# Output weights' operands made in two large tiles of their own, spread over more products, and more gate buffers in the merging

## The chip, the cores and the metric

The kernel runs on one core of a Trainium2 chip. The metric is the device time of one execution in microseconds (us). The time of before is the median of three runs; its profile is one further execution, taken by the hardware profiler.

## The reference

One mixer layer over two sequences (1024 and 256 tokens, width 1024, all float32): a normed and modulated input `h` goes through one wide projection, whose slices feed two branches; the branches are merged by gates and projected once more.

```
p = h @ w_in                         # 1024 -> 11280 columns
y_conv = cb * dwconv3(cc * cx) * silu(cz)
h_fwd, h_bwd = mlstm(q, k, v, gates), the same on the flipped sequence
y_m = sigmoid(o) * headnorm(h_fwd + h_bwd) * silu(mz)
g_conv, g_mlstm = split(sigmoid(gmerge))
merged = g_conv * (y_conv @ w_proj_conv) + g_mlstm * (y_m @ w_proj_mlstm)
y = rms_norm(x + gate * (merged @ w_out))
```

## The kernel before, in words

**Numbers.** The matmuls take float32r operands. To keep float32's accuracy each operand is split into a high part (rounded by a cast) and a low part (what is left), and a product is hi·hi + hi·lo + lo·hi. A split of weights is `split_op`: ACT casts the raw values into `wh` (L319), POOL subtracts to make `wl` (L320). `wh` and `wl` have four buffers each in the pool `wp`, taken in turn: the fifth split gets the first buffer, when what used it is done.

**The order.** The kernel doesn't issue instructions directly. Each piece of work is recorded with `op` (engine, an assumed duration, what it reads and writes, a step, and `low` for work without hurry) on a `Board`. When a stage is written, the board plays all its pieces through a simple model of the engines and issues them in the order of the modelled starts. On the chip each engine (and SP, which issues the DMAs) then works off its own list strictly in order; a piece that is late holds all that stands behind it on that engine. `board.step` says at which product a piece is due.

**The in-projection.** The columns of `w_in` go in pairs of 128-column blocks. A pair is a one-level Strassen product of seven half-size products (moving operands `b11`, `b21`, `t2`, `t3`, `t1`, `t4`, `b22`; the hi and lo parts of these lie in tiles named `b00H`, `b00L`, `b10H`, `t2H`, `xt` and so on); some gate pairs have five after their corners were done first. All stand in the list `todo`: 308 products. `go(k)` issues product k: 24 matmuls of 128x128 by 128x320 into one `acc` (L809; three `acc` buffers in PSUM). `prep(k)` makes its weights some products ahead: raw loads, combinations on DVE (L674), the split. The result is read out of `acc` by DVE (L718) or ACT (L732). `advance(n)` runs `go` for the products from `at[0]` to n and sets `at[0]` to n. `ends[0]` is 77 (the gate pairs and the first head's K, V and Q are done), `ends[1]` 84 (behind the first of eight output-gate pairs, `og`), `ends[2]` 91, `ends[8]` 133; the pairs of the convolution branch follow.

**Beside the products.** Several jobs are put between them, all in this one stage:
- `out_weights` makes the operands for the last projection: it loads `w_out`, forms the seven Strassen combinations, splits them, and stores them in DRAM (`op_dr`, seen in the trace as `b_dr` and `t_dr`) until the end. In before it does so in four steps. Each loads 4 × 256 KB into two tiles of the pool `big` (two buffers), and has eight parts: an ACT cast (L1293, 128x512) into a `wh`, a POOL subtraction (L1294) into a `wl`, and two stores of 256 KB (L1297). DVE makes the combinations in place (L1300). One part is put at each product, from 36 on.
- `gate_inputs` makes the 16 gate columns by a small product of its own (L988, 64 matmuls of 128x32 by 128x320), with both `big` and one `wh`.
- `recurrences` computes the chunk recurrences of the gates, and `weights(i)`, twenty times, loads a row from DRAM (`a_dr`) into a `big`, works on it on POOL and ACT, and stores it (`ex_dr`). The combinations of the convolution pairs use `big` too.

**Merging.** `merge(i, y)` is run for 16 blocks near the end: it loads a gate tile `th` and a tile `zc` of 128x640 (320 KB each), multiplies 24 matmuls per half into a PSUM bank (L1869 to L1871), then DVE multiplies (L619) and adds `zc` (L1877). `th` has three buffers, `zc` two. The raw weights of the blocks come in pairs of loads (`raw`, three buffers), and `b`, `t` tiles of the last projection's operands come back from DRAM in the same queue. `th` tiles are also the landing places in the mLSTM stage before it (L1682) and in `first_ym` and `second_ym`.

The driving loop of the in-projection in before:

```
    beginning()
    advance(31)
    for _ in out_weights():
        advance(at[0] + 1)
    advance(ends[0] - 7)
    board.step = at[0]
    gate_inputs()
```

`out_weights` yields 40 times, so the loop ends with `at[0]` at 71; `advance(70)` then runs nothing and sets it to 70.

Of the kernel before, what the change touches and what calls it, by code (L numbers as in the profile page):

```python
# [9 lines left out]
F32 = mybir.dt.float32  # L10
# [6 lines left out]
P = 128  # L17
# [12 lines left out]
TH2 = T // 2  # L30
TQ = T // 4
SEQS = [(0, 8), (8, 2)]
CB, CC, CX, CZ, CQ, CK, CV, CO, CMZ, CGP, CGM = (
# [7 lines left out]
class Board:  # L41
# [140 lines left out]
def encoder_kernel(  # L182
# [124 lines left out]
    def load(kb, dst, src, r, w, low=False):  # L307
        op("SP", kb, lambda: dma(dst(), src), r=r, w=w, low=low)
# [296 lines left out]
    def big():  # L605

        return buf(rp, [P, T], F32, "big", 2)
# [667 lines left out]
    def out_weights():  # L1275

        for k in range(4):
            places = [big() for _ in range(2)]
            r11, r12, r21, r22 = raws = [((lambda b=places[i % 2], c=i // 2: b[:, c * 512:(c + 1) * 512]), (places[i % 2], i // 2))
                                         for i in (0, 1, 2, 3)]  # L1280
            for i, (ap, tok) in enumerate(raws):
                kt, n0 = k + 4 * (i // 2), 512 * (i % 2)
                load(256, ap, w_out[0, kt * P:(kt + 1) * P, n0:n0 + 512], (), [tok], True)

            for _ in range(1 + 4 * (k == 0)):
                yield

            def parts(nm, x):
                wh, wl = (buf(wp, [P, 4, P], F32R, t, 4) for t in ("wh", "wl"))
                def flat(t):  # L1290
                    return t[:].rearrange("p a b -> p (a b)")

                op("ACT", .63, lambda: A.copy(flat(wh), x[0]()), r=[x[1]], w=[wh])  # L1293
                op("POOL", 1.4, lambda: G.tensor_tensor(out=flat(wl), in0=x[0](), in1=fp(flat(wh)), op=ALU.subtract),  # L1294
                   r=[x[1], wh], w=[wl])
                for i, t in enumerate((wh, wl)):
                    op("SP", 256, lambda i=i, t=t, k=k: dma(op_dr[nm][i, :, k], fp(flat(t))), r=[t], low=True)  # L1297

            def comb(out, x, y, o=ALU.subtract):
                op("DVE", .69, lambda: V.tensor_tensor(out=out[0](), in0=x[0](), in1=y[0](), op=o), r=[x[1], y[1]], w=[out[1]])  # L1300

            yield parts("b22", r22)
            yield parts("b12", r12)
            comb(r22, r22, r12)
            yield parts("t3", r22)
            yield parts("b11", r11)
            comb(r12, r12, r11)
            yield parts("t1", r12)
            yield parts("b21", r21)
            comb(r11, r22, r11, ALU.add)  # L1310
            yield parts("t2", r11)
            comb(r21, r21, r11)
            yield parts("t4", r21)
# [68 lines left out]
    psB = bstack.enter_context(tc.tile_pool(name="psB", bufs=3, space=PSUM))  # L1382
    thp = hpstack.enter_context(tc.tile_pool(name="thp", bufs=3, side="right"))

# [244 lines left out]
    class Filler:  # L1629
# [36 lines left out]
        def unit(self, after):  # L1666
# [6 lines left out]
            if q == 0:  # L1673
                if 0 < i < 2 * KT - 1:
                    self.split(i + 1)
                if i % 2 == 0 and i < 2 * KT - 2:
                    self.load_w(i // 2 + 1)
                if i == KT:
                    self.load_y(1)
                t0 = HBS[b][0]  # L1680
                if i:
                    self.th[i] = buf(thp, [P, TH2], F32, "th", 3)  # L1682
                    load(320, lambda i=i: self.th[i][:], th_dr[n * P:(n + 1) * P, t0:t0 + TH2], (),
                         [(self.th[i], 0), (self.th[i], 1)])
# [21 lines left out]
    def first_ym(n):  # L1706
# [3 lines left out]
        for k in range(4):  # L1710
            raw = buf(thp, [P, TH2], F32, "th", 3)
            kt = 4 * n + k
# [81 lines left out]
    mgp = ctx.enter_context(tc.tile_pool(name="mgp", bufs=1))  # L1794
    zcp = hpstack.enter_context(tc.tile_pool(name="zcp", bufs=2, side="right"))
    banks = []
# [31 lines left out]
    def second_ym(n):  # L1828
        y = [buf(hp, [P, 4, TH2], F32R, ("b00", "b10")[n] + part, 1) for part in "HL"]
        v = ym_dr[:].rearrange("(k p) t -> p k t", p=P)  # L1830
        for k in range(4):
            raw = buf(thp, [P, TH2], F32, "th", 3)
            kt = 4 * n + k
# [464 lines left out]
```

## Time and profile before

| what | us |
|---|---|
| median of 3 runs (1697.9 to 1701.9) | 1698.43 |
| the profiled execution | 1700.25 |
| its span (first to last instruction) | 1698.5 |
| PE busy | 1640.0 |
| DVE, ACT, POOL busy | 1031.7, 584.8, 704.7 |

The stages lie so in the span: preparation to about 87 us, in-projection to about 1180, mLSTM with the convolution branch's projection to about 1460, merging to about 1590, then the last projection. The output weights are made between about 165 and 320.

The profile's page lists busy time, a picture of the span in 40 slices, the chain of work that ended last, and groups of instructions. The views of the trace that are used here: *waits* list, for each engine, what its instructions waited for (total us, times, longest us); *windows* give the busy time of each engine in a stretch, with the clock that TensorE was granted (1.00 is full), the share of time that the DMA engines were busy, and GB/s; the *timeline* gives single instructions with start, length and, in brackets, the idle time ahead of them and what ended it. PE is the matmul part of TensorE, PEld its weight loads.

### The profile page before, as it was taken

Reading aid. Unit: us, or ns where it says so; the run is one execution under the profiler, and the core shown is the slowest. Engines: PE = TensorE matmul, PEld = TensorE weight load, DVE = VectorE, ACT = ScalarE, POOL = GpSimd, SP = SyncE. Lnnn points to the kernel's source line nnn. Section 1 sums busy time; section 2 is a strip of 40 time slices with the busy share of each in tenths; the row PEclk is TensorE's granted clock in tenths of the full one; section 3 lists DMA queues with packets and bytes.
Section 4 is the critical chain, followed back from the end, with each engine's and each line's share of the span. In section 5 each row is a group of like instructions: output and inputs, shape, how many; then the busy total and the mean of one; then the engine's idle time right before and its main releaser. Section 6 shows DMA issues by size and latency. Waiting matters only on the chain.

```text
span 1698.5 us, 28022 instructions
## 1 busy us (share of the span) xinstructions
PE 1640.0 (97%) x10528; PEld 1564.9 (92%) x10528; DVE 1031.7 (61%) x1731; ACT 584.8 (34%) x1142; POOL 704.7 (41%) x514
## 2 busy tenths in 40 slices
PE   6999999899999999999999999999999999999997
PEld 3989998799999999999999999999888899999876
DVE  5785555456645656666565887752147777443587
ACT  4643443124544222222222222121256565321232
POOL 1243665434655466776666643333210002333000
PEclk8999999999999999999999999999999999999999
DMA  9434769523554122222222465557878865795654
GB/s 362 131 98 153 246 225 253 124 83 104 152 149 127 49 74 81 69 61 66 74 69 69 121 148 147 118 128 241 286 237 259 273 196 165 256 325 191 227 190 161
DMA packets 300746, 275.44 MB, mean 162 GB/s; under 512 B 98260, under 2 KB 240836, under 8 KB 300612
## 3 DMA queue, kind: packets, MB, share of 16 engines
q1 hardware_dynamic: 300308, 273.40, 52.2%
q8 instruction: 83, 1.36, 0.3%
q14 instruction: 51, 0.42, 0.1%
q10 hardware_dynamic: 304, 0.27, 0.0%
HBM read 187.94 MB, written 85.66 MB: 161 GB/s over the span
## 4 chain that ended last, share of the span: by engine, by line
PE 75%; DMA 2%; DVE 2%; ACT 1%; SPq 0%; issue 0%; POOL 0%; ACTq 0%; DVEq 0%
PE acc L809 50%; PE u L1486 3%; PE qc L1446 3%; PE acc L1961 2%; PE acc L1962 2%; PE acc L1963 2%; PE acc L1694 2%; PE acc L1693 2%; PE acc L1869 2%; PE acc L1695 2%; PE acc L1870 2%; PE acc L1871 2%; DMA th<-th_dr 1%; PE misc L1569 1%; PE misc L1529 1%; PE acc L988 1%
## 5 line engine op out<-in xcount | busy, mean ns | idle before, releaser
L320 POOL TENSOR_TENSOR wl<-comb,wh 128x512 fp32r<-128x512 f32 x176 | 251.5, 1430 | 257.7 <-ACT wh L319 236.3
L320 POOL TENSOR_TENSOR wl<-raw,wh 128x512 fp32r<-128x512 f32 x169 | 237.8, 1408 | 274.7 <-ACT wh L319 258.9
L718 DVE TENSOR_TENSOR q<-acc,q 128x640 f32<-128x640 f32 x272 | 220.5, 818 | 193.2 <-PE acc L809 185.0
L809 PE MATMUL acc<-xt,wh 128*128 128x320 f32 x1408 | 264.8, 310 | 2.0 <-ACT wh L319 2.0
L809 PEld LDWEIGHTS acc<-xt,wh 128*128 128x128 f32 x1408 | 221.7, 188 | 2.6 <-ACT wh L319 2.5
L319 ACT CAST wh<-raw 128x512 fp32r<-128x512 f32 x169 | 104.2, 619 | 310.6 <-PE acc L809 181.9
L319 ACT CAST wh<-comb 128x512 fp32r<-128x512 f32 x176 | 108.7, 619 | 288.8 <-PE acc L809 235.1
L809 PE MATMUL acc<-xt,wl 128*128 128x320 f32 x704 | 161.2, 310 | 2.4 <-POOL wl L320 2.4
L1652 POOL TENSOR_TENSOR wl<-raw,wh 128x512 fp32r<-128x512 f32 x28 | 36.5, 1307 | 226.6 <-ACT wh L1651 219.5
L809 PEld LDWEIGHTS acc<-xt,wl 128*128 128x128 f32 x704 | 118.1, 188 | 2.9 <-POOL wl L320 2.9
L674 DVE TENSOR_TENSOR comb<-raw 128x512 f32<-128x512 f32 x88 | 79.6, 905 | 59.3 <-DMA raw<-in_w_in_dram 34.6
L877 POOL TENSOR_TENSOR big<-big,q 128x640 f32<-128x640 f32 x48 | 78.3, 1631 | 36.0 <-DVE q L718 27.6
L616 ACT ACTIVATE q<-q,zero 128x640 f32<-128x640 f32 x76 | 63.0, 830 | 79.1 <-DVE q L718 77.7
L619 DVE SCALAR_TENSOR_TENSOR th<-th,acc 128x320 f32<-128x320 f32 x62 | 29.9, 485 | 94.0 <-PE acc L1871 42.9
L809 PE MATMUL acc<-b00H,wh 128*128 128x320 f32 x360 | 85.0, 318 | 1.0 <-ACT wh L319 1.0
L809 PE MATMUL acc<-b00H,wl 128*128 128x320 f32 x360 | 83.1, 312 | 2.6 <-POOL wl L320 2.6
L809 PE MATMUL acc<-t3L,wh 128*128 128x320 f32 x352 | 81.4, 313 | 2.7 <-DVE t3L L371 2.7
L809 PE MATMUL acc<-b00L,wh 128*128 128x320 f32 x360 | 83.2, 313 | 0.0
L809 PE MATMUL acc<-t3H,wh 128*128 128x320 f32 x352 | 81.4, 313 | 1.7 <-ACT t3H L370 1.2
L809 PE MATMUL acc<-t2H,wl 128*128 128x320 f32 x352 | 80.5, 310 | 1.8 <-POOL wl L320 1.8
L809 PE MATMUL acc<-b11H,wl 128*128 128x320 f32 x352 | 80.3, 309 | 1.5 <-POOL wl L320 1.5
L809 PE MATMUL acc<-b11H,wh 128*128 128x320 f32 x352 | 81.3, 312 | 0.5 <-ACT wh L319 0.5
(392 smaller groups left out, 4127.7 us busy)
## 6 DMA issues: line engine op xcount, KB each, us to landing
raw<-in_w_in_dram SPq DMA_DIRECT2D x120, 256.0 KB
raw<-in_w_in_dram SPq DMA_DIRECT2D x36, 512.0 KB
th<-th_dr SPq DMA_DIRECT2D x31, 320.0 KB
th_dr<-q SPq DMA_DIRECT2D x28, 320.0 KB
raw<-in_w_proj_conv_dram SPq DMA_DIRECT2D x16, 512.0 KB
raw<-in_w_proj_mlstm_dram SPq DMA_DIRECT2D x16, 512.0 KB
late<-t_dr SPq DMA_DIRECT2D x16, 512.0 KB
k<-kn_dr SPq DMA_DIRECT2D x56, 128.0 KB
```

The lines of the kernel that those rows point to most:

```text
L319: op("ACT", .63, lambda: A.copy(wh[:], src()), r=r, w=[wh])
L320: op("POOL", 1.4, lambda: G.tensor_tensor(out=wl[:], in0=src(), in1=fp(wh[:]), op=ALU.subtract), r=[*r, wh], w=[wl])
L616: A.activation(out, in_, AF.Tanh, bias=zero[:, 0:1], scale=0.5)
L674: op("DVE", .9, lambda: V.tensor_tensor(out=t[:], in0=x(), in1=y(), op=o), r=[x.tok, y.tok], w=[t])
L718: op("DVE", .82, lambda: V.tensor_tensor(out=two(dst()), in0=acc[:, :, 0:TQ], in1=two(t()), op=ALU.add), r=[acc, t.tok], w=[dst.tok])
L809: PE.matmul(acc[:, q, 0:TQ], st_[:, k_, :], m_[:, q * TQ:(q + 1) * TQ], start=k_ == 0 and n == 0, stop=k_ == 3 and n == 2)
L877: op("POOL", 1.65, lambda: G.tensor_tensor(out=dst(), in0=dst(), in1=t(), op=ALU.mult), r=[dst.tok, t.tok], w=[dst.tok])
L1446: PE.matmul(pq[:, 0:HD + 2], qTs[i][:, kd, c * P:(c + 1) * P], C[:, kd, :], start=kd == 0, stop=kd == 1)
L1486: PE.matmul(pu[:, db, 0:HD + 2], k[:, db * P:(db + 1) * P], wv[:], start=True, stop=True)
L1652: op("POOL", 1.36, lambda wh=wh, wl=wl, src=src: G.tensor_tensor(out=wl[:], in0=src(), in1=fp(wh[:]), op=ALU.subtract), r=[raw, wh], w=[wl])
L1693: PE.matmul(acc[:, :TQ], wh, yH, start=kt == 0, stop=False)
L1694: PE.matmul(acc[:, :TQ], wh, yL, start=False, stop=False)
```

## The change

- `out_weights` takes two `big` once and keeps them to its end, as ten slots of 256 columns: four for raw values, six for results as three (hi, lo) pairs, (5, 6), (7, 8) and (4, 9), used in turn. It works in eight chunks of half the columns; a part is an ACT cast (L1298) and a POOL subtraction (L1299) of 128x256 between slots, and one store of 256 KB for two neighbouring slots (L1303) or two of 128 KB (L1307). There are 64 parts, 32 loads of 128 KB and 85 stores, all marked `low`. No `wh` or `wl` is used. One chunk is recorded at a time, over products 31 to 81.
- The gate product moves from product 70 to `ends[1]` (84), `recurrences` from `ends[0]` to `ends[2]` (91). The twenty `weights(i)` are spread over the og pairs 4 to 7, not 2 to 7. Product 70 is issued once.
- `th` has five buffers (`NTH`), and `zc` in the merging five.

Lines behind L31 are one line further down in the changed kernel, those behind `out_weights` 14.

```
     def out_weights():
-        for k in range(4):
-            places = [big() for _ in range(2)]
...
+        places = [big() for _ in range(2)]
+
+        def slot(i):
+            b, c = places[i // 5], i % 5
+            return (lambda: b[:, c * 256:(c + 1) * 256]), (b, c)
+
+        raws, turns = [slot(i) for i in range(4)], [0]
+        outs = [(5, 6), (7, 8), (4, 9)]
+
+        def chunk(k, n):
+            r11, r12, r21, r22 = raws
             for i, (ap, tok) in enumerate(raws):
-                kt, n0 = k + 4 * (i // 2), 512 * (i % 2)
-                load(256, ap, w_out[0, kt * P:(kt + 1) * P, n0:n0 + 512], (), [tok], True)
-            for _ in range(1 + 4 * (k == 0)):
-                yield
+                kt, n0 = k + 4 * (i // 2), 512 * (i % 2) + 256 * n
+                load(128, ap, w_out[0, kt * P:(kt + 1) * P, n0:n0 + 256], (), [tok], True)
             def parts(nm, x):
-                wh, wl = (buf(wp, [P, 4, P], F32R, t, 4) for t in ("wh", "wl"))
...
-                op("ACT", .63, lambda: A.copy(flat(wh), x[0]()), r=[x[1]], w=[wh])
-                op("POOL", 1.4, lambda: G.tensor_tensor(out=flat(wl), in0=x[0](), in1=fp(flat(wh)), op=ALU.subtract),
-                   r=[x[1], wh], w=[wl])
-                for i, t in enumerate((wh, wl)):
-                    op("SP", 256, lambda i=i, t=t, k=k: dma(op_dr[nm][i, :, k], fp(flat(t))), r=[t], low=True)
+                hi, lo = outs[turns[0] % 3]
+                turns[0] += 1
+                (h, ht), (l, lt) = slot(hi), slot(lo)
+                cs = slice(256 * n, 256 * n + 256)
+                op("ACT", .38, lambda: A.copy(h().bitcast(F32R), x[0]()), r=[x[1]], w=[ht], low=True)
+                op("POOL", .8, lambda: G.tensor_tensor(out=l().bitcast(F32R), in0=x[0](), in1=h(), op=ALU.subtract),
+                   r=[x[1], ht], w=[lt], low=True)
+                if lo == hi + 1:
+                    b, c = ht
+                    op("SP", 256, lambda: dma(op_dr[nm][:, :, k, cs].rearrange("i p c -> p i c"),
+                                              b[:, c * 256:(c + 2) * 256].rearrange("p (i c) -> p i c", i=2)), r=[ht, lt], low=True)
+                else:
+                    for i, (ap, tok) in enumerate(((h, ht), (l, lt))):
+                        op("SP", 128, lambda i=i, ap=ap: dma(op_dr[nm][i, :, k, cs], ap()), r=[tok], low=True)
...
+        for i in range(8):
+            yield chunk(i // 2, i % 2)
...
-    for _ in out_weights():
-        advance(at[0] + 1)
-    advance(ends[0] - 7)
+    for i, _ in enumerate(out_weights()):
+        advance(31 + (ends[1] - 34) * (i + 1) // 8)
+    advance(ends[1])
     board.step = at[0]
     gate_inputs()
-    advance(ends[0])
+    advance(ends[2])
     board.step = at[0]
     recurrences()
-    for n in range(KT):
-        if n > 1:
+    for n in range(2, KT):
+        if n > 3:
             for i in range(NH * NC // 2):
-                if i * 6 // (NH * NC // 2) == n - 2:
-                    board.step = at[0] + 7 * (i * 6 % (NH * NC // 2)) // (NH * NC // 2)
+                if i * 4 // (NH * NC // 2) == n - 4:
+                    board.step = at[0] + 7 * (i * 4 % (NH * NC // 2)) // (NH * NC // 2)
                     weights(i)
...
-        th, zc = buf(thp, [P, TH2], F32, "th", 3), buf(zcp, [P, TH2], F32, "zc", 2)
+        th, zc = buf(thp, [P, TH2], F32, "th", NTH), buf(zcp, [P, TH2], F32, "zc", 5)
```

How the change moves instructions is seen at three places. The first is ACT, between products 60 and 70. Before, casts for the output weights (L1293, from `big` into `wh`) and main casts (L319, from `raw` or `comb` into `wh`) take the four `wh` in turn:

```order
L319 CAST wh<-raw 128x512
L1293 CAST wh<-big 128x512
L319 CAST wh<-raw 128x512
L1293 CAST wh<-big 128x512
L732 COPY q<-acc 128x640
L319 CAST wh<-comb 128x512
L1293 CAST wh<-big 128x512
L319 CAST wh<-comb 128x512
```

and now, at the same part of the work, with L320 the main cast and L1298 the one for the output weights, within the two `big`:

```order
L1298 CAST big<-big 128x256
L320 CAST wh<-comb 128x512
L1298 CAST big<-big 128x256 x2
L320 CAST wh<-raw 128x512
L1298 CAST big<-big 128x256
L320 CAST wh<-raw 128x512
L1298 CAST big<-big 128x256 x3
L320 CAST wh<-comb 128x512 x2
L1298 CAST big<-big 128x256 x2
```

The output casts are half as wide and write none of the `wh`, and stand between the main casts as before, one to three at a time.

The second is PE just ahead of the gate product, before (L988, 32 rows out) behind a product with `b00` (L809):

```order
L809 MATMUL acc<-b00H,wh 128x320 x2
L809 MATMUL acc<-b00L,wh 128x320 x2
L809 MATMUL acc<-b00H,wl 128x320 x2
L988 MATMUL acc<-b00H,wh 32x320 x2
L988 MATMUL acc<-b00L,wh 32x320 x2
```

and now, later in the list (L810 is the product, L989 the gate):

```order
L810 MATMUL acc<-b11H,wh 128x320 x2
L810 MATMUL acc<-b11L,wh 128x320 x2
L810 MATMUL acc<-b11H,wl 128x320 x2
L989 MATMUL acc<-b00H,wh 32x320 x2
L989 MATMUL acc<-b00L,wh 32x320 x2
```

In both a product with `b00` stands behind the gate; before, that is product 70 again, whose first turn stands just ahead of the gate, and now it is product 84 after product 83 with `b11`.

The third is SP at the start of the merging, where the loads of `zc`, raw weights, `th` and the `b` operands follow each other; before:

```order
L1704 DMA zc_dr<-th 128x640
L308 DMA zc<-zc_dr 128x640
L308 DMA raw<-in_w_proj_mlstm_dram 128x4x256
L308 DMA zc<-zc_dr 128x640
L308 DMA raw<-in_w_proj_mlstm_dram 128x4x256 x2
L308 DMA th<-ym_dr 128x640 x3
```

and now:

```order
L1718 DMA zc_dr<-th 128x640
L309 DMA zc<-zc_dr 128x640
L309 DMA raw<-in_w_proj_mlstm_dram 128x4x256
L309 DMA zc<-zc_dr 128x640 x4
L309 DMA raw<-in_w_proj_mlstm_dram 128x4x256 x2
L309 DMA th<-ym_dr 128x640 x4
```

Three more `zc` loads stand ahead of the second and third of the `raw` loads.

More of the change, by code (lines that the diff above doesn't have):

```diff
@@ L1299, in comb @@
             def comb(out, x, y, o=ALU.subtract):
-                op("DVE", .69, lambda: V.tensor_tensor(out=out[0](), in0=x[0](), in1=y[0](), op=o), r=[x[1], y[1]], w=[out[1]])
-            yield parts("b22", r22)
-            yield parts("b12", r12)
+                op("DVE", .42, lambda: V.tensor_tensor(out=out[0](), in0=x[0](), in1=y[0](), op=o), r=[x[1], y[1]], w=[out[1]],
+                   low=True)
+            parts("b22", r22)
+            parts("b12", r12)
             comb(r22, r22, r12)
-            yield parts("t3", r22)
@@ L1710, in first_ym @@
         for k in range(4):
-            raw = buf(thp, [P, TH2], F32, "th", 3)
+            raw = buf(thp, [P, TH2], F32, "th", NTH)
             kt = 4 * n + k
@@ L1794, in encoder_kernel @@
     mgp = ctx.enter_context(tc.tile_pool(name="mgp", bufs=1))
-    zcp = hpstack.enter_context(tc.tile_pool(name="zcp", bufs=2, side="right"))
+    zcp = hpstack.enter_context(tc.tile_pool(name="zcp", bufs=5, side="right"))
     banks = []
@@ L1831, in second_ym @@
         for k in range(4):
-            raw = buf(thp, [P, TH2], F32, "th", 3)
+            raw = buf(thp, [P, TH2], F32, "th", NTH)
             kt = 4 * n + k
```

20 lines of the change are left out of this document (9 added, 11 removed).

## The prediction

> **What bounds the kernel now.** I read the page's busy times and chain first, then the waits of TensorE over the span, then stretches of the time in which they fall, then what the engines there wait for. The page:
>
> ```profile
> span 1698.5 us, 28022 instructions
> PE 1640.0 (97%) x10528; PEld 1564.9 (92%) x10528; DVE 1031.7 (61%) x1731; ACT 584.8 (34%) x1142; POOL 704.7 (41%) x514
> ```
>
> TensorE (PE) is busy 97% of the span, so only two things can shorten it: fewer matmuls, or fewer of the 58 us in which it does none. All waits of PE, longest sums first (total, times, longest):
>
> ```profile
> PE acc L809 <- POOL wl L320: 8.8, 10, 1.7
> PE acc L1869 <- DVE th L619: 6.2, 10, 1.0
> PE acc L809 <- ACT wh L319: 5.2, 6, 1.4
> ...
> PE acc L1693 <- DVE th L619: 3.8, 1, 3.8
> ```
>
> The products of the in-projection (L809) wait 14.0 us for their weights' high and low parts. The stretches show where (length, then busy time and count for PE, PEld, DVE, ACT, POOL; granted clock, DMA share, GB/s):
>
> ```profile
> 100.00:180.00 80.00, 80.00 (x544) 80.00 (x543) 46.71 (x59) 27.83 (x42) 32.82 (x23) 0.99 0.47 149
> 180.00:233.00 53.00, 52.03 (x354) 51.54 (x352) 31.64 (x30) 22.70 (x37) 37.98 (x27) 1.00 0.74 249
> 233.00:319.00 86.00, 72.96 (x461) 69.05 (x462) 47.30 (x50) 25.70 (x44) 50.68 (x38) 0.98 0.75 216
> 319.00:345.00 26.00, 25.89 (x171) 23.16 (x171) 7.99 (x20) 5.86 (x10) 7.95 (x6) 0.93 0.47 100
> ```
>
> In 100 to 180 a matmul takes 80.00/544 = 0.147 us, and a product of 24 of them 3.53 us. At that rate the 461 of 233 to 319 need 67.8 us, and took 86: 18.2 lost. The 354 of 180 to 233 lost 0.9, and the clock of 0.93 in 319 to 345 cost 26 × 0.07 = 1.8. Together 20.9 us, all while the output weights are made. (A matmul record that is missing counts 0.15 us too much.)
>
> What ScalarE (ACT) does there, start and length:
>
> ```profile
> 286.56 0.62 ACT L1293 CAST wh<-big 128x512 fp32r<-128x512 f32 x1 [2.06 <-issue]
> 291.26 0.62 ACT L319 CAST wh<-comb 128x512 fp32r<-128x512 f32 x1 [4.08 <-PE acc L809]
> 296.27 0.62 ACT L1293 CAST wh<-big 128x512 fp32r<-128x512 f32 x1 [4.39 <-PE acc L809]
> 296.80 0.61 ACT L319 CAST wh<-comb 128x512 fp32r<-128x512 f32 x1
> ```
>
> The cast for the output weights (L1293) at 296.27 waited for a product to leave its `wh`; the main cast (L319) came behind it, and the product that needs this `wh` started with a wait. A main cast every second turn of four buffers means that only two products' halves are ever ahead.
>
> **Output weights: off the main buffers.** The 32 splits (128x512) become 64 (128x256), none of which takes a `wh` or `wl`. The main splits then have four pairs instead of about two, and the coupling by turns is gone. GpSimd (POOL) load: the row of the output splits in 233 to 319 is
>
> ```profile
> L1294 POOL TENSOR_TENSOR wl<-big,wh 128x512 fp32r<-128x512 f32 x17 | 23.9, 1406 | 21.5 <-ACT wh L1293 21.0 <-PE acc L809 0.5
> ```
>
> So 50.68 - 23.9 = 26.8 us of main splits over 461/24 = 19.2 products, 1.39 a product. The new splits, at half the elements, are 0.70 (bounds: 0.70, and 1.41 if width did not matter), 64 of them over the 50 products from 31 to 81: 0.90 a product. 2.29 of 3.53 is 65%, below the 37.98/53 = 72% of 180 to 233, where PE lost only 0.94 us in 53. So I take as what stays that rate over 50 × 3.53 = 176.5 us: 3.1 us. Gain 20.9 - 3.1 = 17.8.
>
> Part of the 20.9 is a lower clock. Four slices of PE (busy, clock, DMA share, GB/s):
>
> ```profile
> 295.00:300.00 5.00, 2.82 (x17) 0.90 0.99 264
> 300.00:305.00 5.00, 4.02 (x20) 0.76 0.46 121
> ...
> 315.00:320.00 5.00, 2.37 (x13) 0.95 0.65 130
> 320.00:325.00 5.00, 5.00 (x27) 0.71 0.91 194
> ```
>
> 5 × (0.10 + 0.24 + 0.05 + 0.29) = 3.4 us. Each drop stands in or right behind a slice in which PE was half idle, so I count it as going with the waits. The Trainium skill (TensorE: Matmul & The Clock Gate, "What's actually happening") has the clock halved after at least one idle window of about 3.4 us; the longest wait here is 1.7 us, so read to the letter these drops had another cause and would stay, which is a rival below. The trace speaks against the letter: the drops are there only where waits are dense.
>
> **One product fewer.** The loop over the output weights of before runs to product 70, then the position is set back, and product 70 is issued again behind the gate product. The page's groups and the PE timeline:
>
> ```profile
> L809 PE MATMUL acc<-b00H,wh 128*128 128x320 f32 x360 | 85.0, 318 | 1.0 <-ACT wh L319 1.0
> ...
> L809 PE MATMUL acc<-t3H,wh 128*128 128x320 f32 x352 | 81.4, 313 | 1.7 <-ACT t3H L370 1.2
> ```
> ```profile
> 323.07 0.45 PE L809 MATMUL acc<-b00H,wl 128*128 128x320 f32 x2
> 323.36 0.45 PE L988 MATMUL acc<-b00H,wh 128*32 128x320 f32 x2
> ...
> 332.42 0.46 PE L988 MATMUL acc<-b11L,wh 128*32 128x320 f32 x2
> 332.72 0.46 PE L809 MATMUL acc<-b00H,wh 128*128 128x320 f32 x2
> ```
>
> 360 is 8 matmuls each of 45 products, 352 of 44: one `b00` too many, on both sides of the gate (L988). The change never sets back: 3.5 us of PE, nothing hides it, plus a split and raw loads off the path.
>
> **DMA and slots.** The bytes stay (4 MB in, 16 MB out), in rows half as long. New: three (hi, lo) slots used in turn, each held until its store has landed. Nearest rows, an output store on SP and the cast that waited for it:
>
> ```profile
> 260.24 0.44 SPq L1297 DMA_DIRECT2D b_dr<-wh  x1
> ```
> ```profile
> 265.29 0.62 ACT L319 CAST wh<-comb 128x512 fp32r<-128x512 f32 x1 [3.58 <-DMA b_dr<-wh]
> ```
>
> 5.05 us from issue to release. A slot's cycle is 0.31 (half a cast) + 0.70 + 5.05 = 6.1 us plus waits in three queues; 64 parts over three slots are 21.3 cycles, and 176.5/21.3 = 8.3 us are to be had. 2.2 us a cycle are left for queues. What they took before, on SP (total, times, longest):
>
> ```profile
> SPq L1297 <- ACT wh L1293: 36.9, 18, 6.6
> SPq L1297 <- POOL wl L1294: 18.5, 13, 2.3
> ```
>
> SP waited 2.0 and 1.4 us each time. So it fits, narrowly; priced at nothing, with what happens otherwise as a rival. The Trainium skill (DMA: Bandwidth & Descriptors, "Latency and other measured facts") puts the fixed cost of a DMA at some 2 us; by that a cycle would be about 3 us shorter and this rival would have no ground. The 5.05 us say otherwise, under a DMA share of 0.75.
>
> **Gate and recurrences later, `weights` denser.** The gate product costs the same PE time at step 84 as at 70 (no wait stands at 323.36 or 332.72); it needs both `big`, so it now stands behind the last output store, issued some products earlier: zero, or the 5 us of one store if it is not. The 20 `weights` (two per round) go from 42 products into 28. One round on SP:
>
> ```profile
> 417.62 0.98 SPq L308 DMA_DIRECT2D big<-a_dr  x2
> ...
> 425.66 0.34 SPq L311 DMA_DIRECT2D ex_dr<-big  x1
> ...
> 428.83 4.44 SPq L308 DMA_DIRECT2D big<-a_dr  x2
> ```
>
> 11.2 us, so ten rounds are 112 us against 28 × 3.53 = 98.8. They run over by 13 us, past the og pairs; the next to want a `big` are the conv pairs right behind. Priced at nothing, since a late round first eats the waits in its own chain and the three `acc` (about two products, 7 us); the rest is a rival.
>
> **Merging: five `th` and `zc`.** Its PE waits are the 6.2 us above: 0.6 us each in ten blocks, on the multiply (L619) of the block's first half, which the order puts behind part 0 of the second half. No buffer is waited for, and in the changed order eleven blocks stand so: +0.6. In the stretch
>
> ```profile
> 1464.00:1480.00 16.00, 16.00 (x111) 16.00 (x110) 4.41 (x6) 6.48 (x11) 7.17 (x6) 1.00 0.93 332
> ```
>
> DMA is 93% busy, and three more `zc` (3 × 328 kB, 3.0 us at 332 GB/s) go ahead of the raw weights of the third block: up to +3 if these are late. In the mLSTM stage PE waits once for `th` (3.8 us, L1693); with more `th` buffers that may go or double: 0, bounds ±3.8.
>
> **Sum.** -17.8 - 3.5 + 0.6 = -20.7 us. The profiled execution took 1700.25 us (span 1698.5 and 1.75 around it) and would take 1679.5. The median of the runs, 1698.43, is 1.8 lower: 1677.7.
>
> **Rivals.**
> (1) The slots are the new bound. With 2.7 us of queues instead of 2.2 the cycle is 8.8, 21.3 × 8.8 = 187.4, 10.9 us over what is to be had. Output casts that wait for a slot hold the main casts behind them in ACT's order, so PE loses it: in place of the 3.1, -24.4 + 0.6 + 10.9 = -12.9, 1685.5. For: DMA is 0.75 busy, and a faster PE asks for the same main bytes in less time. Against: four main pairs cover two products more than before.
> (2) Slower: the same mechanism with a cycle of 9.8 us, a store landing in 6.5 us and 2.2 of queues. 208.7 - 176.5 = 32.2 lost, +8.4: 1706.8. It decides from 9.4 us on, where the loss is the 23.8 us gained. For: the DMA share of 0.99 in 295 to 300. Against: even in 228 to 324, with more output work per product, the longest wait for a store (last number) was
>
> ```profile
> ACT wh L319 <- DMA b_dr<-wh: 7.3, 2, 3.7
> ```
>
> (3) `weights` run into the conv pairs: 13.2 - 7.1 = 6.1 lost, 1683.8. For: the count above. Against: where they stand now, ACT is 51% and POOL 61% busy and PE never stops, so a round has air in it:
>
> ```profile
> 402.00:531.00 129.00, 129.00 (x881) 129.00 (x880) 73.83 (x79) 65.53 (x143) 78.76 (x56) 1.00 0.54 147
> ```
>
> (4) The clock drops stay, by the skill's letter: 3.4 less gained, 1681.1.
> (5) The change doesn't do what it says: the waits come from stores and loads in SP's queue, not from shared `wh`, and move with the output work. Then -3.5 + 0.6: 1695.5. For: ACT also waits for stores (3.58 above). Against: the 4.08 and 4.39 are waits for PE.
>
> **Numbers.** Forecast 0.53, (1) 0.18, (2) 0.05, (3) 0.12, (4) 0.05, (5) 0.07. A measurement here tells a difference from about 0.3%, 5.1 us. Faster: 0.53 + 0.18 + 0.12 + 0.05 = 0.88; same 0.07; slower 0.05. The low end is the forecast without the 3.1 that stays and with the mLSTM's 3.8 gone: 1677.7 - 6.9 = 1670.8, say 1671. The high end takes in (3), (4) and (1) up to a cycle of 9.0 (15.2 lost, 1689.8): 1690. Outside are (2), (5) and the worst of (1), under 2 in 10.
>
> **What would show it.** Right: L809 has 24 matmuls fewer (`b00H,wh` x352); from 228 us on products follow each 3.53 us, the L809 waits for `wh` and `wl` fall from 14.0 to some 3 us and the clock stays 1.00; the gate runs with no wait; the waits in the merging's product (L1869 of before) read 11 times 0.6. Rival (1) or (2) would show as ACT L1298 waiting for stores ahead of an L320 cast, with PE waiting for `wh`; (3) as PE waiting at L810 after the og pairs, with DVE waiting for a `big`. I am wrong if the products between 31 and 81 still lose over 8 us, or if the time is above 1690.

## The result and the profile after

The changed kernel takes 1681.54 us (median of four runs, 1680.08 to 1683.68), before 1700.16 us in the runs beside it (1697.9 to 1703.7): a ratio of 0.989, 95% interval 0.9866 to 0.9914. Forecast were 1677.7 us, 0.988 of before; the range was 1671 to 1690. The profiled execution took 1680.08 us, 20.2 less than that of before.

The page of the changed kernel, its span and busy times:

```profile
span 1678.3 us, 28164 instructions
PE 1628.0 (97%) x10504; PEld 1556.4 (93%) x10504; DVE 1026.3 (61%) x1747; ACT 587.0 (35%) x1172; POOL 700.4 (42%) x545
```

The same stretches as before (length, busy time and count for PE, PEld, DVE, ACT, POOL; clock, DMA share, GB/s), and two further ones:

```profile
180.00:233.00 53.00, 53.00 (x363) 53.00 (x363) 31.64 (x37) 25.26 (x49) 37.00 (x38) 1.00 0.75 242
233.00:319.00 86.00, 86.00 (x588) 86.00 (x587) 49.40 (x63) 30.31 (x63) 57.67 (x57) 1.00 0.87 235
319.00:345.00 26.00, 26.00 (x179) 26.00 (x178) 11.66 (x18) 7.91 (x15) 12.69 (x11) 1.00 0.43 127
345.00:400.00 55.00, 55.00 (x382) 52.17 (x381) 33.66 (x63) 16.40 (x25) 18.09 (x14) 1.00 0.20 62
400.00:540.00 140.00, 135.14 (x905) 133.66 (x904) 78.36 (x101) 62.15 (x135) 72.07 (x54) 0.99 0.45 126
```

From 180 to 400 TensorE doesn't wait at all and its clock is full: 588 matmuls in the 86 us in which before had 461. The loss is in the last row: 905 matmuls at 0.147 us are 133.0 us, so 7.0 of the 140 are lost, where before lost nothing. The waits of PE over the span:

```profile
PE acc L1883 <- DVE th L620: 6.4, 11, 0.6
PE acc L810 <- DVE q L719: 5.0, 4, 3.4
...
PE acc L1707 <- DVE th L620: 2.8, 1, 2.8
```

The two L809 groups that summed to 14.0 us are gone. L1883 is the merging (11 waits of 0.6). New is the second row: products wait for DVE to read out an `acc` (L719).

Where the 20.2 us came from is read from the first start of each later stage, before and after. These are the rows of the stages' first matmul lines (durations, then first to last start): the mLSTM stage's, the merging's and the last projection's.

Before:

```profile
L1693 PE MATMUL acc<-b00H,wh x128: 305/309/753, 1179.6 to 1461.8; 128*128 128x320 f32 x128
L1869 PE MATMUL acc<-y,wh x128: 303/309/417, 1464.0 to 1522.1; 128*128 128x320 f32 x128
L1961 PE MATMUL acc<-b,wh x48: 391/394/498, 1585.7 to 1677.5; 128*128 128x512 f32 x48
```

After:

```profile
L1707 PE MATMUL acc<-b00H,wh x128: 305/309/503, 1162.8 to 1441.4; 128*128 128x320 f32 x128
L1883 PE MATMUL acc<-y,wh x128: 302/309/419, 1443.6 to 1502.2; 128*128 128x320 f32 x128
L1975 PE MATMUL acc<-b,wh x48: 392/394/501, 1565.7 to 1657.5; 128*128 128x512 f32 x48
```

Up to the mLSTM stage 16.8 us are gained; that stage gains 3.6 more; the merging gives 0.4 back; the rest is the same within 0.2.

### The profile page after: what moved, and what is told of

Its sections match the earlier page's. It is cut to its first block, busy times and chain, and to the rows that moved or that the text cites. A ratio compares the mean times of both kernels' runs of the same rounds, so it can differ in the third digit from the quotient of the medians.

```text
span 1678.3 us, 28164 instructions
## 1 busy us (share of the span) xinstructions
PE 1628.0 (97%) x10504; PEld 1556.4 (93%) x10504; DVE 1026.3 (61%) x1747; ACT 587.0 (35%) x1172; POOL 700.4 (42%) x545
## 4 chain that ended last, share of the span: by engine, by line
PE 87%; DMA 5%; DVE 3%; issue 1%; ACT 1%; SPq 1%; POOL 1%; DVEq 0%; POOLq 0%; ACTq 0%
PE acc L810 59%; PE u L1500 3%; PE qc L1460 3%; PE acc L1883 2%; PE acc L1885 2%; PE acc L1884 2%; PE acc L1975 2%; PE acc L1977 2%; PE acc L1976 2%; PE acc L1708 2%; PE acc L1707 2%; PE acc L1709 2%; DMA raw<-in_w_in_dram 2%; PE misc L1583 1%; PE misc L1543 1%
## 5 line engine op out<-in xcount | busy, mean ns | idle before, releaser
L321 POOL TENSOR_TENSOR wl<-comb,wh 128x512 fp32r<-128x512 f32 x176 | 246.5, 1401 | 243.8 <-ACT wh L320 223.5
L321 POOL TENSOR_TENSOR wl<-raw,wh 128x512 fp32r<-128x512 f32 x168 | 233.5, 1391 | 274.4 <-ACT wh L320 269.1
L719 DVE TENSOR_TENSOR q<-acc,q 128x640 f32<-128x640 f32 x272 | 220.6, 818 | 185.8 <-PE acc L810 175.4
L810 PE MATMUL acc<-xt,wh 128*128 128x320 f32 x1408 | 263.9, 309 | 0.0
L810 PEld LDWEIGHTS acc<-xt,wh 128*128 128x128 f32 x1408 | 220.9, 188 | 0.1
L320 ACT CAST wh<-raw 128x512 fp32r<-128x512 f32 x168 | 103.7, 619 | 319.5 <-PE acc L810 184.4
L320 ACT CAST wh<-comb 128x512 fp32r<-128x512 f32 x176 | 108.8, 619 | 271.8 <-PE acc L810 237.9
L810 PE MATMUL acc<-xt,wl 128*128 128x320 f32 x704 | 160.5, 309 | 0.0
L1666 POOL TENSOR_TENSOR wl<-raw,wh 128x512 fp32r<-128x512 f32 x28 | 36.0, 1288 | 227.4 <-ACT wh L1665 219.0
L810 PEld LDWEIGHTS acc<-xt,wl 128*128 128x128 f32 x704 | 117.7, 188 | 0.0
L675 DVE TENSOR_TENSOR comb<-raw 128x512 f32<-128x512 f32 x88 | 72.9, 829 | 65.4 <-DMA raw<-in_w_in_dram 41.6
L810 PE MATMUL acc<-b10H,wh 128*128 128x320 f32 x352 | 81.4, 313 | 3.4 <-DVE q L719 3.4
L810 PE MATMUL acc<-t3L,wh 128*128 128x320 f32 x352 | 81.2, 312 | 2.7 <-DVE t3L L372 2.7
L675 DVE TENSOR_TENSOR comb<-raw,comb 128x512 f32<-128x512 f32 x44 | 48.1, 1092 | 58.2 <-POOL wl L321 58.2
L810 PE MATMUL acc<-t3H,wh 128*128 128x320 f32 x352 | 81.2, 312 | 1.4 <-ACT t3H L371 1.4
L810 PE MATMUL acc<-b00H,wh 128*128 128x320 f32 x352 | 82.5, 316 | 0.0
L810 PE MATMUL acc<-t2H,wh 128*128 128x320 f32 x352 | 80.5, 310 | 1.6 <-DVE q L719 1.6
L810 PE MATMUL acc<-t3H,wl 128*128 128x320 f32 x352 | 81.1, 312 | 0.1
L810 PE MATMUL acc<-b11H,wh 128*128 128x320 f32 x352 | 81.2, 312 | 0.0
```

The costliest lines, as they stand in the source:

```text
L320: op("ACT", .63, lambda: A.copy(wh[:], src()), r=r, w=[wh])
L321: op("POOL", 1.4, lambda: G.tensor_tensor(out=wl[:], in0=src(), in1=fp(wh[:]), op=ALU.subtract), r=[*r, wh], w=[wl])
L675: op("DVE", .9, lambda: V.tensor_tensor(out=t[:], in0=x(), in1=y(), op=o), r=[x.tok, y.tok], w=[t])
L719: op("DVE", .82, lambda: V.tensor_tensor(out=two(dst()), in0=acc[:, :, 0:TQ], in1=two(t()), op=ALU.add), r=[acc, t.tok], w=[dst.tok])
L810: PE.matmul(acc[:, q, 0:TQ], st_[:, k_, :], m_[:, q * TQ:(q + 1) * TQ], start=k_ == 0 and n == 0, stop=k_ == 3 and n == 2)
L1666: op("POOL", 1.36, lambda wh=wh, wl=wl, src=src: G.tensor_tensor(out=wl[:], in0=src(), in1=fp(wh[:]), op=ALU.subtract), r=[raw, wh], w=[wl])
```

## The experiments

The theory: the products waited because output splits and main splits took the same four `wh` and `wl` in turn; own places cure this. The product 70 that was issued twice costs its own time. The new waits at 460 to 520 come from the twenty `weights` being denser. Rivals: the wider spread, the half width and low priority, or a lighter load on the engines cures the waits; the slots take the place of the shared buffers as the bound.

### Product 70 once

Before, with one line changed:

```
-        advance(at[0] + 1)
+        advance(min(at[0] + 1, ends[0] - 7))
```

> Before, with product 70 issued once (24 matmuls fewer) and nothing else changed. Theory: the product stands behind the gate product, where TensorE is busy without a wait, so its 3.5 us come off whole: 3.5 us faster than before, ratio 0.998, L809 waits still about 14 us. Rival: the weights of the next products are late there, so the time goes into waits: 0 to 1 us faster, with waits of some 17 us.

1693.36 us, 0.996 of before (0.9946 to 0.9975): 6.9 us, of which the product explains 3.5. The waits in its trace between 180 and 345 us:

```profile
PE acc L809 <- POOL wl L320: 6.6, 7, 1.5
PE acc L809 <- ACT wh L319: 3.3, 4, 1.4
PE acc L988 <- DVE wh L976: 0.5, 1, 0.5
```

9.9 us and not 14.0, from one trace of each kernel. With the product's own time, 4.1 us of waits went too, by one split fewer in the turns or by the order that follows from it. Which of these two isn't told apart. The rival (the time goes into waits) is out.

### Only the wider spread

The changed kernel, but its `out_weights` is the function of before (32 parts of 128x512 in `wh` and `wl`), with

```
-        advance(31 + (ends[1] - 34) * (i + 1) // 8)
+        advance(31 + (ends[1] - 34) * (i + 1) // 40)
```

> The changed kernel with before's making of the output weights (32 parts of 128x512 through the shared wh and wl), spread over products 31 to 81 as in the changed kernel. Theory (the shared turns of wh and wl made the waits): at least half of the 20.9 us lost between 180 and 345 stays, so 10 to 20 us slower than the changed kernel, 0.995 to 1.000 of before. Rival (the load per product made the waits, and the wider spread cures it): the waits are gone here too, the time is the changed kernel's within 3 us, 0.988 to 0.991 of before.

1700.3 us, 0.9996 (0.998 to 1.0012): no gain. The waits from 180 to 345 us:

```profile
PE acc L810 <- POOL wl L321: 6.6, 9, 1.4
PE acc L810 <- ACT wh L320: 4.3, 8, 1.0
```

10.9 of the 14.0 us are still there. The spread is truly wider on the chip: the output casts start from 174.7 to 345.6 us, over 170.9 us, where before they took 141.0 (174.1 to 315.1). And POOL has no more work per product than in the changed kernel: 93.23 us in 180 to 345 for 1001 matmuls, 2.24 us a product, against 107.36 for 1126, 2.29. The waits of the `weights` come on top (4.0 us for L719, 1.6 for L1250), which eats the 3.5 of the product. The wider spread is not the cure.

### Half width, low priority and spread, in the shared buffers

The changed kernel, with its 64 parts in the first 256 columns of the shared `wh` and `wl`, a part recorded at a time (the first one six steps behind the first loads) and each part stored by two DMAs of 128 KB (the code is cut):

```
-                hi, lo = outs[turns[0] % 3]
-                turns[0] += 1
-                (h, ht), (l, lt) = slot(hi), slot(lo)
+                wh, wl = (buf(wp, [P, 4, P], F32R, t, 4) for t in ("wh", "wl"))
...
-        advance(31 + (ends[1] - 34) * (i + 1) // 8)
+        advance(31 + (ends[1] - 34) * (i + 1) // 70)
```

> The changed kernel with its half-width parts, their low priority and their spread kept, but cast and subtracted into the first 256 columns of the shared wh and wl, not into the two tiles. Theory (the shared turns are the cause): the products' waits for wh and wl between 180 and 345 us are back, 10 us or more, and it is 10 to 30 us slower than the changed kernel, 0.995 to 1.01 of before. Rival (half width, low priority and spread cure it, not the places): under 3 us of such waits, within 3 us of the changed kernel.

1707.6 us, 1.0048 (1.0032 to 1.0065), slower than before. The stretch of this run, and of the changed kernel's first trace, in the same columns as above:

```profile
180.00:345.00 165.00, 146.56 (x942) 141.05 (x942) 82.28 (x100) 56.33 (x113) 96.57 (x96) 0.98 0.68 196
```
```profile
180.00:345.00 165.00, 165.00 (x1126) 165.00 (x1126) 92.70 (x115) 63.47 (x125) 107.36 (x105) 1.00 0.76 220
```

and the waits of this run there:

```profile
PE acc L810 <- POOL wl L321: 15.0, 15, 1.8
PE acc L810 <- ACT wh L320: 3.4, 6, 0.8
```

18.4 us of waits while POOL is 59% busy (96.57 of 165), below the 65% at which the changed kernel has none. Per product this is 2.46 us, a little more than there; but the run before has the waits at 2.24. What ACT waits for shows the coupling, in this run and in the changed kernel:

```profile
ACT wh L1302 <- PE acc L810: 27.4, 12, 5.0
ACT wh L320 <- DMA b_dr<-wh: 9.2, 5, 3.1
```
```profile
ACT big L1298 <- DMA b_dr<-big: 18.2, 9, 3.4
ACT big L1298 <- DMA t_dr<-big: 12.4, 8, 3.9
```

In the shared buffers an output cast (L1302) waits for a product to leave its `wh`, and a main cast (L320) for an output store to leave its own. In the changed kernel only the output casts (L1298) wait for output stores; no main cast does, and no output cast waits for a product. That more parts mean more turns between two main splits, and so fewer main splits ahead, is how I read the larger sum here. It is the turns, not the load: this run and the one before it settle it together. (`wh` and `wl` of their own for the output weights, beside the shared four, were not tried.)

### Only the places

The changed kernel with before's spread, gate product at 70, recurrences at 77 and `weights` over og pairs 2 to 7:

```
-        advance(31 + (ends[1] - 34) * (i + 1) // 8)
-    advance(ends[1])
+        advance(31 + (ends[0] - 7 - 31) * (i + 1) // 8)
+    advance(ends[0] - 7)
```

> The changed kernel with its own places for the output weights, but before's spread: made by product 70, gate product at 70, recurrences at 77, the twenty weights over og pairs 2 to 7; product 70 issued once. Theory: own places cure the waits also at the closer spread, and the new waits of the changed kernel between 460 and 520 us (about 6.8 us with the lower clock) are not there, since the weights have 42 products again: 5 to 7 us faster than the changed kernel, 0.985 to 0.986 of before. Rival (slots bound): 64 parts over 39 products leave 6.5 us a slot cycle; if a cycle takes 8 us, some 30 us are lost and it is slower than before, 1.00 to 1.01.

1697.46 us, 0.9986 (0.9973 to 0.9998), where 0.985 was expected. The waits of PE between 290 and 345 us, and DVE there:

```profile
PE acc L989 <- DVE wh L977: 22.3, 1, 22.3
```
```profile
319.72 0.23 DVE L976 CAST wh<-big 128x128 fp32r<-128x128 f32 x1 [4.83 <-DMA big<-in_w_in_dram]
319.98 1.23 DVE L977 TENSOR_TENSOR wh<-big,wh 128x128 fp32r<-128x128 f32 x1
```

No product (L810) waits; nearly all of the loss is one wait at the gate product (L989), whose raw weights need a `big`. (Behind it the clock is low for a while, 0.50 in 320 to 325 us.) The tiles are held until the last output stores. The casts show how long that is:

```profile
L1298 ACT CAST big<-big x64: 387/406/408, 169.8 to 316.1; 128x256 fp32r<-128x256 f32 x64
```

146.3 us for 64 parts in three slots, 21.3 cycles of 6.9 us; the 39 products from 31 to 70 are only 137.6. So the chain of slots was too long for this spread: its casts waited 31.6 us for output stores. But the products went on, and the gate paid. And no wait of the `weights` is in this trace.

### The close spread with the late gate

The changed kernel, with one line:

```
-        advance(31 + (ends[1] - 34) * (i + 1) // 8)
+        advance(31 + (ends[0] - 7 - 31) * (i + 1) // 8)
```

> The changed kernel with the output weights recorded over products 31 to 70, as close as in before, and everything else as changed (gate product at 84). Theory: own places alone cure the waits of the products; the later gate is needed only because the tiles are held until the last output store, about 6.9 us per slot cycle and 146 us for all; so no wait in the in-projection up to 345 us, and within 2 us of the changed kernel. Rival (the wider spread itself removes waits): 3 us or more of waits of the products between 230 and 345 us, and 4 us or more slower than the changed kernel.

1680.25 us, 0.9893 (0.9878 to 0.9908); the changed kernel, run again beside it, 1682.63, 0.991 (0.9895 to 0.9925). They are 2.4 us apart, where I had said 2, and the intervals overlap. From 180 to 345 us PE has no wait in its trace. But the spread is closer in the order of recording alone. These are the output casts of the changed kernel and of this run:

```profile
L1298 ACT CAST big<-big x64: 387/406/410, 169.8 to 325.3; 128x256 fp32r<-128x256 f32 x64
```
```profile
L1298 ACT CAST big<-big x64: 389/407/409, 168.4 to 324.5; 128x256 fp32r<-128x256 f32 x64
```

They stand alike, so this run can't tell a close spread from a wide one. Two others can: in "Only the wider spread" the casts took 170.9 us in shared buffers, and the waits stayed; in "Only the places" they took 146.3 us in places of their own, and no product waited. So the wider spread is not what cures the waits; what the change needed with the places is the later gate. (In "Only the places" the recurrences and the `weights` stand earlier too, but its loss stands at the gate.)

### Two slots, not three

```
-        outs = [(5, 6), (7, 8), (4, 9)]
+        outs = [(5, 6), (7, 8)]
...
-                hi, lo = outs[turns[0] % 3]
+                hi, lo = outs[turns[0] % 2]
```

> The changed kernel with two (hi, lo) slots in turn for the output weights, not three. Theory (a slot is held until its store has landed, 6.9 us a cycle as in the run with the close spread): 32 cycles are 219 us, the last cast stands at about 390 us, the gate product waits about 45 us for the tiles: 1.01 to 1.02 of before. Rival (the chain goes at the pace of the order and a cycle can be shorter): under 5.5 us a cycle, no wait at the gate, within 3 us of the changed kernel.

1707.9 us, 1.0041 (1.0026 to 1.0057), where 1.01 to 1.02 was expected. Its casts and its wait:

```profile
L1298 ACT CAST big<-big x64: 388/404/408, 169.7 to 367.8; 128x256 fp32r<-128x256 f32 x64
```
```profile
PE acc L989 <- DVE wh L977: 24.9, 1, 24.9
```

198.1 us over 32 cycles are 6.2 us each: less than the 6.9 that I took over from three slots, so the wait is 25 and not 45. Why a cycle is shorter here isn't shown. The number of slots bounds the chain: two take 198.1 us, three 155.5 with the same recording. Up to 400 us PE again waits at the gate only.

### The changed kernel again

> The changed kernel once more, as the measure for the three beside it: 1680 to 1684 us, 0.987 to 0.991 of before, with 4 to 6 us of waits between 460 and 520 us. Rival: those waits were a chance of one execution, and are gone in this one.

1682.63 us. In its trace the waits are there again, at 467, 494 and 518 us, the longest 3.2 us, so they are not chance:

```profile
PE acc L810 <- DVE q L719: 4.3, 3, 3.2
...
PE acc L810 <- ACT big L1250: 1.2, 1, 1.2
```

What makes the longest is seen in the changed kernel's first trace. SP, POOL, ACT and DVE:

```profile
507.55 0.36 SPq L309 DMA_DIRECT2D big<-a_dr  x1
508.11 0.92 SPq L309 DMA_DIRECT2D raw<-in_w_in_dram  x2
```
```profile
513.59 1.27 POOL L1246 TENSOR_TENSOR big<-big,masks 128x512 f32<-128x512 f32 x1 [5.50 <-DMA big<-a_dr]
```
```profile
514.89 1.28 ACT L1250 ACTIVATE big<-big,gcol 128x128 f32<-128x128 f32 x4 [6.99 <-POOL big L1246]
```
```profile
515.20 1.43 DVE L675 TENSOR_TENSOR comb<-raw 128x512 f32<-128x512 f32 x1 [6.43 <-DMA raw<-in_w_in_dram]
516.55 0.81 DVE L719 TENSOR_TENSOR q<-acc,q 128x640 f32<-128x640 f32 x1
```

The load of one of the `weights` and the raw loads are issued together at 507.6 and 508.1, and land some 6 and 7 us later. POOL waits for the first, ACT for POOL, DVE for the raw weights, and the read-out of an `acc` (L719) stands behind that on DVE. The raw loads themselves were late on SP: it issued nothing from 496.8 to 503.6, as the next raw load waited 6.8 us for a main subtraction (L321) to leave its buffer, and on POOL that stood behind an operation of the `weights` (L1246), which had waited 3.0 us for its own load. PE has run out of `acc` by then and starts again behind it:

```profile
517.51 0.87 PE L810 MATMUL acc<-b10H,wh 128*128 128x320 f32 x2 [3.42 <-DVE q L719]
```

### The `weights` over five og pairs

The changed kernel with

```
-        if n > 3:
+        if n > 2:
             for i in range(NH * NC // 2):
-                if i * 4 // (NH * NC // 2) == n - 4:
+                if i * 5 // (NH * NC // 2) == n - 3:
```

> The changed kernel with the twenty weights over the og pairs 3 to 7 (four to each seven products), not 4 to 7 (five). Theory: the waits of the changed kernel between 460 and 520 us come from five rounds' worth per pair in queues that are worked off in order; with four they are gone, PE is without a wait from 100 to 540, and the time is 5 to 7 us under the changed kernel's, 0.985 to 0.986 of before. Rival (the order alone, not the density, makes the wait): still 3 us or more of waits there, and the time within 2 us of the changed kernel's.

1677.69 us, 0.9879 (0.9865 to 0.9892), 4.9 us under the changed kernel beside it. The stretch (PE alone) in the changed kernel's second run and here:

```profile
460.00:540.00 80.00, 75.02 (x498) 0.98 0.56 143
```
```profile
460.00:540.00 80.00, 76.74 (x518) 1.00 0.56 145
```

498 matmuls at 0.147 us are 73.2, so 6.8 us were lost; 518 are 76.1, so 3.9. The waits are down from 5.0 (0.50, 1.24 and 3.24 us) to 3.2 us (the longest 1.7), and the clock drop is gone; by these two traces 2.9 us are gained here. So it matters over how many products the `weights` are recorded, as the time says; but the waits were to be gone, and are not.

On the chip the `weights` are not denser at all. This is their work on ACT, before and in the changed kernel:

```profile
L1249 ACT ACTIVATE big<-big,gcol x80: 383/388/406, 410.0 to 530.7; 128x128 f32<-128x128 f32 x80
```
```profile
L1250 ACT ACTIVATE big<-big,gcol x80: 384/387/407, 434.7 to 554.8; 128x128 f32<-128x128 f32 x80
```

120.7 and 120.1 us, and 114.5 in this run. What differs is the order: recorded over 28 products (98.8 us) they stand among main work that is ready before they are. That this is the whole cause isn't shown.

### Four places for the `weights`

The changed kernel, two of the `weights` in each `big`:

```
-        place = big()
+        if i == 0:
+            wts.extend(big() for _ in range(2))
+        b, c = wts[i % 2], i // 2 % 2
+        place = (b, c)
```

> The changed kernel with the same density of weights, but two of them in each big tile (four places, not two, both tiles held to the end). Theory in its narrower form (a round is bound by the time from the store of one to the landing of the next load in the same place): four places hide that time, the waits between 460 and 520 us are gone, 5 to 7 us under the changed kernel's, 0.985 to 0.986 of before. Rival (the work per product on ACT and POOL is what is too dense): waits as in the changed kernel, within 2 us of it.

1682.8 us, 0.9906 (0.9892 to 0.992), the same as the changed kernel; a wait of 5.1 us for L719 stands in its trace. The twenty `weights` now take 77.1 us on ACT and not 120.1, so the turn of the tiles is what set their pace; but it is not what makes PE wait. What is left is the reading of the trace above, loads whose users stand in the engines' orders before they land; no run tests it by itself.

### The gate early, the `weights` over 42 products

The changed kernel with the close spread, the gate at product 80, the recurrences at 86 and `weights` over og pairs 2 to 7:

```
-    advance(ends[1])
+    advance(ends[0] + 3)
     board.step = at[0]
     gate_inputs()
-    advance(ends[2])
+    advance(ends[1] + 2)
...
-                if i * 4 // (NH * NC // 2) == n - 4:
+                if i * 6 // (NH * NC // 2) == n - 2:
```

> The changed kernel with the output weights over products 31 to 70, the gate product at 80, recurrences at 86 and the twenty weights over og pairs 2 to 7 as in before. Theory: the tiles are free at about product 78 (the last output cast stood at 316 us where the spread was this close), so the gate waits for less than 2 us, and with 42 products for the weights the waits between 460 and 550 us are gone: 4 to 7 us under the changed kernel, 0.984 to 0.987 of before, the fastest so far. Rival: the gate still waits for the tiles, 5 us or more at L989, and the time is not under the changed kernel's.

1678.57 us, 0.9879 (0.9858 to 0.9899), where 0.984 to 0.987 was expected. The gate waits for nothing, 180 to 345 us runs at full rate; in 460 to 560 waits of 3.7 us remain. (The last output cast stands at 325.2 us, not at 316.) By the ratio to before it is as fast as the run with five og pairs, and no faster: waits stay with 42 products too, though before and "Only the places" had none with 42.

### The merging's buffers

The changed kernel with three `th` and two `zc`:

```
-NTH = 5
+NTH = 3
...
-        th, zc = buf(thp, [P, TH2], F32, "th", NTH), buf(zcp, [P, TH2], F32, "zc", 5)
+        th, zc = buf(thp, [P, TH2], F32, "th", NTH), buf(zcp, [P, TH2], F32, "zc", 2)
```

> The changed kernel with three th buffers and two zc, as before. Theory: no wait of TensorE hung on these buffers; within 1.5 us of the changed kernel, 0.988 to 0.990 of before, with ten or eleven waits of 0.6 us in the merging. Rival: the buffers saved 2 us or more in the mLSTM stage and the merging; then 2 to 4 us slower than the changed kernel, 0.990 to 0.992.

1684.59 us, 0.9908 (0.9887 to 0.9929). That lies in the rival's range, but can't be told from the changed kernel's 0.989 and 0.991. In the merging its trace has

```profile
PE acc L1883 <- DVE th L620: 8.8, 11, 2.6
```

eleven waits, one of 2.6 us in place of 0.6. Product 70 issued once, which has the old buffers too, shows the like:

```profile
PE acc L1869 <- DVE th L619: 8.3, 10, 3.1
```

The profile of before happens to have none above 1.0. All ten traces with five buffers have 6.4 to 6.6 us in this row, no wait above 0.8. What stands ahead of the long wait in the trace of this run, on DVE and PE:

```profile
1494.52 0.90 DVE L1891 TENSOR_TENSOR mg<-th,zc 128x320 f32<-128x320 f32 x2 [1.52 <-DMA zc<-zc_dr]
1495.38 0.49 DVE L620 SCALAR_TENSOR_TENSOR th<-th,acc 128x320 f32<-128x320 f32 x1
```
```profile
1495.92 0.41 PE L1883 MATMUL acc<-y,wh 128*128 128x320 f32 x1 [2.56 <-DVE th L620]
```

DVE waits for a `zc` that lands late, the multiply stands behind it, and PE waits for that. With two `zc` the addition waits for its load in all three traces (4.5 us before, 2.1 and 3.5), with five in none (in two of those ten the multiply has one wait of 1.9 us for a `zc`). So few buffers let a late load through to PE in two of three executions here, for 2 to 3 us.

## Why the prediction was right, and where it was not

- **What bound the kernel: right.** The 20.9 us lost between 180 and 345 belong to the shared `wh` and `wl`. The runs with the shared buffers (10.9 and 18.4 us of waits) and those with places of their own (none) show it.
- **What stays of it: wrong, on the safe side.** I let 3.1 us stay, at the rate of 180 to 233 before. POOL came to the 65% that I had worked out (107.36 of 165 us), and nothing stays. In 180 to 233 itself POOL is 70% busy now (37.00 of 53 us; 72% before), and nothing is lost: that rate was the work of the shared turns, not of the load. A half-width subtraction takes 0.82 us in the mean (0.74 in the median), nearer to the 0.70 that I took than to the other bound, 1.41.
- **One product fewer: right**, 3.5 us; `b00H,wh` is x352 in the page after. The run with this alone gains 6.9, since waits went with it; in my sum these waits are part of the 17.8.
- **The slots: right in price, narrowly.** A cycle worked out at 6.1 us plus queues is 7.3 in the changed kernel (155.5 us over 21.3 cycles); 8.3 were to be had. (The comparison with a fixed cost of a DMA decides nothing, as the 5.05 us hold the transfer of 256 KB as well.) Rivals (1) and (2) didn't come up. But their mechanism was wrong: in the two runs in which the chain was late it did not hold the products, it held the tiles and so the gate, 22.3 and 24.9 us in one piece.
- **The gate: right at 84.** For the case that it comes too early I had 5 us; with the old place (70) it was 22.3. The later gate is a needed part of the change.
- **`weights`: wrong.** I priced them at nothing and rival (3) at 6.1 us; the changed kernel loses 7.0 there, in 4.8 us of waits and the clock behind them. The count was near: ten rounds at 11.2 us are 112, and they took 120.1. The step that failed is that "a late round first eats the waits in its own chain". In the trace it doesn't: the parts of a round stand in the same orders as the main work, and where their loads land late, DVE comes late to the read-out of `acc`. Also the place was wrong; it is among the og pairs, not in the conv pairs.
- **The clock: as forecast.** Rival (4) was that the drops of 3.4 us stay. From 180 to 400 the clock is now 1.00. In the run with half-width parts in the shared buffers the waits are back and the clock falls again, with no wait over 1.8 us. PE alone, 325 to 340 us (length, busy, clock, DMA share, GB/s):

```profile
325.00:330.00 5.00, 3.94 (x18) 0.69 0.62 161
330.00:335.00 5.00, 2.75 (x13) 0.84 0.43 138
335.00:340.00 5.00, 4.42 (x22) 0.79 0.09 32
```

- **The merging: right**, eleven waits in place of ten, and 0.4 us. "No buffer is waited for" holds for PE only: DVE waited 4.5 us for `zc` in before, up to 3.5 at once.
- **The sum.** -20.9 - 3.5 + 7.0 = -17.4 up to the mLSTM stage, against 16.8 measured there. Then -3.6 in the mLSTM stage, which I had left at zero with bounds of 3.8. It is no work of the change that can be shown: from the stage's first matmul (L1707) to the first of the merging the changed kernel's first trace takes 280.8 us, its second 285.1, before 284.4. All traces lie between 279.2 and 285.1, and the other two with three `th` at 280.6 and 281.2. So that the profiled 20.2 came so near the forecast 20.7 is in part luck: two misses that partly cancel, 3.1 too little gained and 7.0 too little paid, and 3.6 of chance. The medians differ by 18.6.

## What to carry to other kernels

When two streams of work take the same few buffers in turn, the one that is in no hurry sets how far ahead the other can be; count turns, not load, and give the patient stream a place of its own. A place that is held for long moves the cost to whoever needs that tile next: find that consumer before, and move it behind the last store. And work that is recorded over fewer steps than it takes can cost, even with the engines that do it far from full, when its instructions wait for loads in orders that the main work shares. Last, look in the trace where work of low priority ended up: the order in which it is recorded doesn't say.

## What was unexpected of the hardware

The lower clock (0.69 to 0.84) came with many short waits, none over 1.8 us: in slices of 5 us in which PE was 55 to 88% busy in the run with half-width parts in the shared buffers. Another slice of that run, 64% busy, stayed at 1.00:

```profile
290.00:295.00 5.00, 3.20 (x20) 1.00 0.29 85
```

The one wait of 22.3 us in "Only the places" brought it to 0.50 (305 to 325 us). How long a stretch decides, and by what share, these runs don't tell. A DMA share of 0.87 over 86 us held nothing up, where 0.75 with waits had looked like a bound. And the same program's mLSTM stage took 280.8 and 285.1 us in two executions, at clocks of 1.00 and 0.99: a difference as large as some of those above that one would like to explain.
